# Rotating 96 images by 180 degrees: the third load split into 112 and 16 rows, and a store of the first group tied to it

## The chip, the cores and the metric

The kernel runs on one core of a Trainium2 chip. The metric is the device time of one execution in microseconds; the median of three runs before the change is 121.94 us (121.81 to 122.52).

## The reference

```python
def setup_inputs():
    batch, c, h, w = 32, 3, 256, 256
    return {"x": np.random.randn(batch, c, h, w).astype(np.float32)}

def reference(x):
    return np.rot90(x, k=2, axes=(-2, -1)).astype(np.float32)
```

Each of the 96 images of 256 x 256 floats is turned by 180 degrees. Seen as one row of 65,536 numbers, an image is simply reversed. Nothing is calculated; 25.2 MB are read and 25.2 MB written.

## The kernel before

Every image is cut into four pieces of E = 16,384 numbers (64 KB). The 384 pieces are the rows that the kernel handles, 128 at a time, one to a partition of the on-chip memory. There are three groups (lines 34 and 35): A takes the even pieces of the first 64 images, B the odd ones, C all pieces of the last 32 images. Each group has its own tile of 128 x 16,384 floats, and all three fit at once.

Reversing an image takes two steps. The order of its pieces is reversed by the address pattern of the store (line 54, `::-1`). Inside a piece VectorE reverses the numbers in place: `swap` (lines 56 to 60) exchanges a block of w columns near the front with its mirror image near the back, through the spare tile T, by three copies that read backwards (`back`, line 43). `turn(t, lo, hi)` (line 69) does the swaps for the front columns lo to hi, J = 2048 columns at a time; turning the columns 0 to half = 8192 turns the whole tile. So a tile takes four swaps, twelve copies.

The order of the work is written out by hand. All copies stay in program order on VectorE (line 47). The transfers are issued from two queues: SP issues the loads of A and C and all four stores, in the order written; ACT issues the load of B, after a small clearing of B's first 256 columns by VectorE (line 65), which only delays that load. [...]

- Loads (lines 64 to 67): A on SP, B on ACT, C on SP.
- VectorE turns the columns 0 to 6144 of A (line 76), outermost first. The columns 0 to 256 of A (`LEAD`) are final after the first swap and are stored by a small transfer of 128 KB (line 77).
- Columns 0 to 2560 (`MID`) of B are turned (line 78), then the innermost 2048 of A (line 79). Then the rest of A can be stored (line 80, 8064 KB).
- The rest of B is turned and B stored (lines 81 and 82), then C (lines 83 and 84).

## Time and profile before

| | |
|---|---|
| median of 3 runs | 121.94 us |
| the profiled execution's own time | 121.9 us |
| its span (first to last instruction) | 120.1 us |
| VectorE busy | 44.9 us, 40 instructions |
| DMA | 1008 packets, 50.33 MB |
| VectorE waits for the load of A | 38.3 us |

In the table of slices the span is cut into 40 parts of 3 us; a digit is the busy share in tenths. "DMA" there is the mean of the core's 16 DMA engines. The last part of the page lists the DMA issues: the issuing queue (SPq, ACTq), the size of a store, and the microseconds from the issue to the landing of the last byte. In the timeline each line begins with the start and the length in microseconds; for SPq and ACTq that is the issue alone, not the transfer.

### The profile page before, as it was taken

Reading aid. Unit: us, or ns where it says so; the run is one execution under the profiler, and the core shown is the slowest. Engines: PE = TensorE matmul, PEld = TensorE weight load, DVE = VectorE, ACT = ScalarE, POOL = GpSimd, SP = SyncE. Lnnn points to the kernel's source line nnn. Section 1 sums busy time; section 2 is a strip of 40 time slices with the busy share of each in tenths; the row PEclk is TensorE's granted clock in tenths of the full one; section 3 lists DMA queues with packets and bytes.
Section 4 is the critical chain, followed back from the end, with each engine's and each line's share of the span. In section 5 each row is a group of like instructions: output and inputs, shape, how many; then the busy total and the mean of one; then the engine's idle time right before and its main releaser. Section 6 shows DMA issues by size and latency. Waiting matters only on the chain.

```text
span 120.1 us, 97 instructions
## 1 busy us (share of the span) xinstructions
DVE 44.9 (37%) x40; POOL 0.2 (0%) x4
## 2 busy tenths in 40 slices
DVE  0000000000000899999999999999400000000000
POOL 0000000000000000000000000000000000000000
DMA  9888988898889988998899777988898889888980
GB/s 349 349 349 371 677 349 349 349 698 349 349 349 633 415 349 349 546 502 349 349 387 687 344 344 344 687 349 349 349 698 349 349 349 698 349 349 349 677 371 0
DMA packets 1008, 50.33 MB, mean 419 GB/s; under 512 B 112, under 2 KB 240, under 8 KB 240
## 3 DMA queue, kind: packets, MB, share of 16 engines
q1 hardware_dynamic: 864, 41.94, 81.3%
q10 hardware_dynamic: 144, 8.39, 16.1%
HBM read 25.17 MB, written 25.17 MB: 419 GB/s over the span
## 4 chain that ended last, share of the span: by engine, by line
DVE 38%; DMA 32%; issue 1%
DMA A<-in_x_dram 32%; DVE T L47 13%; DVE Bt L47 9%; DVE A L47 8%; DVE Ct L47 8%
## 5 line engine op out<-in xcount | busy, mean ns | idle before, releaser
L47 DVE COPY T<-A 128x2048 f32<-128x2048 f32 x4 | 4.9, 1226 | 38.4 <-DMA A<-in_x_dram 38.3
L47 DVE COPY T<-Bt 128x2048 f32<-128x2048 f32 (+2 forms) x5 | 5.1, 1014 | 0.2
L47 DVE COPY Bt<-T 128x2048 f32<-128x2048 f32 (+2 forms) x5 | 5.1, 1014 | 0.2
L47 DVE COPY Bt<-Bt 128x2048 f32<-128x2048 f32 (+2 forms) x5 | 5.1, 1013 | 0.2
L47 DVE COPY T<-Ct 128x2048 f32<-128x2048 f32 x4 | 4.9, 1227 | 0.1
L47 DVE COPY Ct<-T 128x2048 f32<-128x2048 f32 x4 | 4.9, 1227 | 0.1
L47 DVE COPY A<-T 128x2048 f32<-128x2048 f32 x4 | 4.9, 1227 | 0.1
L47 DVE COPY A<-A 128x2048 f32<-128x2048 f32 x4 | 4.9, 1227 | 0.1
L47 DVE COPY Ct<-Ct 128x2048 f32<-128x2048 f32 x4 | 4.9, 1226 | 0.1
L65 DVE MEMSET Bt<- 128x256 f32 x1 | 0.3, 272 | 0.9 <-PEq L99 0.9
L99 POOL MEMSET const-bfloat16-1.0<- 128x1 bf16 x1 | 0.1, 102 | 0.0
L99 POOL MEMSET const-uint8-127<- 128x1 uint8 x1 | 0.1, 102 | 0.0
L99 POOL MEMSET const-float32-0.0<- 128x1 f32 x1 | 0.1, 99 | 0.2 <-issue 0.2
L99 POOL MEMSET const-float32-1.0<- 128x1 f32 x1 | 0.1, 99 | 0.0
## 6 DMA issues: line engine op xcount, KB each, us to landing
out_dram<-A SPq DMA_DIRECT2D x1, 8064.0 KB, 20.9
out_dram<-A SPq DMA_DIRECT2D x1, 128.0 KB, 18.4
A<-in_x_dram SPq DMA_DIRECT2D x1, 38.7
Bt<-in_x_dram ACTq DMA_DIRECT2D x1, 43.1
Ct<-in_x_dram SPq DMA_DIRECT2D x1, 60.1
out_dram<-Bt SPq DMA_DIRECT2D x1, 29.6
out_dram<-Ct SPq DMA_DIRECT2D x1, 33.9
```

The costliest lines, as they stand in the source:

```text
L47: tc.keep_in_program_order(nc.vector.tensor_copy(out=dst, in_=src))
L65: nc.vector.memset(Bt[:, 0:256], 0.0)
L99: nc = _bacc.Bacc("TRN2", target_bir_lowering=False, num_devices=1)
```

## The change

```diff
-    MID = 2560
+    R = P - 16
     LEAD = 256
+    LATE = 6144
+    KEY = 128
     load(A, 0, 0, E)
     nc.vector.memset(Bt[:, 0:256], 0.0)
     load(Bt, 1, 0, E, nc.scalar)
-    load(Ct, 2, 0, E)
+    nc.sync.dma_start(out=Ct[0:R, :], in_=x4[2][0:R, :])
+    nc.sync.dma_start(out=Ct[R:P, :], in_=x4[2][R:P, :])
...
-    turn(A, 0, half - J)
+    turn(A, 0, half - KEY)
     store(A, 0, 0, LEAD)
-    turn(Bt, 0, MID)
-    turn(A, half - J, half)
+    turn(Bt, 0, half - LATE)
+    copy(T[0:R, 0:8], back(Ct, 0, 8)[0:R])
+    turn(A, half - KEY, half)
     store(A, 0, LEAD, E)
-    turn(Bt, MID, half)
+    turn(Bt, half - LATE, half)
     store(Bt, 1, 0, E)
```

The load of C becomes two transfers on SP, one behind the other: partitions 0 to 111, then 112 to 127. VectorE now turns all of A but its innermost 128 columns, then one block of 2048 columns of B. Then it copies eight columns of C's first 112 rows into T. Nobody uses these values; the copy can only run once the 112 rows have landed, and since VectorE works in order, what stands behind it waits as well. Behind it come the innermost 128 columns of A, and with them the store of the rest of A. The remaining 6144 columns of B follow. The number of columns turned is the same; the block of 512 columns and that of 1536 in B are gone, and in A there are one of 1920 and one of 128 in place of one of 2048. The stores and the other loads are unchanged.

## The prediction

> **What bounds the kernel now.** I read the page's top first: which of the units is never at rest.

> ```profile
> span 120.1 us, 97 instructions
> DVE 44.9 (37%) x40; POOL 0.2 (0%) x4
> ...
> DVE  0000000000000899999999999999400000000000
> ...
> DMA  9888988898889988998899777988898889888980
> ...
> DMA packets 1008, 50.33 MB, mean 419 GB/s; under 512 B 112, under 2 KB 240, under 8 KB 240
> ```

> VectorE works 44.9 us, in the middle third. The DMA engines are busy in every slice but the last. So the transfers are the bound, and the question for any edit is whether it lengthens them or leaves a hole between them. Next the DMA issues, which say how long each took to land:

> ```profile
> out_dram<-A SPq DMA_DIRECT2D x1, 8064.0 KB, 20.9
> out_dram<-A SPq DMA_DIRECT2D x1, 128.0 KB, 18.4
> A<-in_x_dram SPq DMA_DIRECT2D x1, 38.7
> Bt<-in_x_dram ACTq DMA_DIRECT2D x1, 43.1
> Ct<-in_x_dram SPq DMA_DIRECT2D x1, 60.1
> out_dram<-Bt SPq DMA_DIRECT2D x1, 29.6
> out_dram<-Ct SPq DMA_DIRECT2D x1, 33.9
> ```

> Added to the issue times of the timeline (columns: start, length; the second fence is a closer look at it):

> ```profile
> 0.73 0.38 SPq L50 DMA_DIRECT2D A<-in_x_dram  x1
> ...
> 1.16 0.43 SPq L50 DMA_DIRECT2D Ct<-in_x_dram  x1
> 39.47 1.23 DVE L47 COPY T<-A 128x2048 f32<-128x2048 f32 x1 [38.34 <-DMA A<-in_x_dram]
> ...
> 54.60 0.43 DVE L47 COPY T<-Bt 128x512 f32<-128x512 f32 x1
> ...
> 70.31 0.54 SPq L53 DMA_DIRECT2D out_dram<-Bt  x1
> ...
> 85.45 0.54 SPq L53 DMA_DIRECT2D out_dram<-Ct  x1
> ```

> ```profile
> 59.76 0.55 SPq L53 DMA_DIRECT2D out_dram<-A  x1
> ```

> they give the landings: A 39.4, B 44.3, C 61.3, A's first 256 columns 61.7 (43.25 + 18.4), the rest of A 80.7, B's store 99.9, C's store 119.4. The last two are 19.2 and 19.5 us apart. A group is 128 rows of 64 KB, eight to each of 16 engines, so one row takes one engine 19.35 / 8 = 2.42 us (27.1 bytes per ns); I call that a slot. The program has 384 rows in and 384 out, 48 slots, 116.2 of the 120.1 us; 3.9 us are the start, the end and the small store. The rows of C are the last eight slots of the loads: 61.3 - 8 x 2.42 = 41.9 to 61.3. After them the stores run without a hole: 61.3 to 119.4 is 58.1 us, 24 slots.

> **The change, part by part.** The sum is made against the profiled execution: 121.9 us, of which 1.8 lie around its span of 120.1; the median of the runs is 121.94, the same.

> *One more issue on SP.* It costs 0.38 to 0.43 us at 1.6 us. SP is next needed at 43.25 for the small store, which still depends only on the first swap of A. Cost nothing, covered by 41 us. One more completion mark per engine: the small store's nine packets per engine took about 61.7 - 61.3 = 0.4 us, so a packet costs 0.04 us at most; taken as 0.

> *The order on VectorE.* A wide copy takes 1.23 us, 1.26 with its gap; 2048 columns against 512 are 1.23 against 0.43, so 0.52 us per 1000 columns over 0.16. Three wide swaps of A end at 50.82 as now. The new 1920-column swap is 3 x (1.16 + 0.03) = 3.6, to 54.4; one swap of B, 3 x 1.26, to 58.2. There VectorE now waits for the 112 rows. The small copy has no row of its own size: between 0 and the 0.43 of 512 columns; I take 0.2, near the 0.16 left at no columns. The 128-column swap is 3 x (0.23 + 0.03) = 0.8. So the large store of A is issued 1.0 us after the 112 rows land, or at 59.2 if they are early. Behind the waiting copy stand three swaps of B (11.35 us) and all of C (15.1 us); behind the store on SP stand those of B and C.

> *The 112 rows and the 16.* Seven rows to each engine, then one. If a row costs 2.42 us wherever it goes, they land at 58.8 and 61.3 and nothing is added. But no row shows a transfer that is narrower than 128 partitions, and this decides everything. What the rows do show: load and store run at the same pace, with one queue filled or two, in every full-width transfer. Their common side is the tile memory, and the pace of all 16 engines together, 434 bytes per ns, is nowhere exceeded. [...] The 16 late rows lie side by side. They could use 16 ways (one slot, no cost) or as few as two (eight rows on each, eight slots, 19.4 us). The no-cost end is a rival below; of the shared cases, 8, 4 and 2 ways, I take the middle, four ways with four late rows on each: four slots, 9.7 us instead of 2.42. Then the 12 other ways carry eight rows each of the 112, so these need eight slots instead of seven, however they are dealt out: 61.3 instead of 58.8, and up to a slot more where two engines meet on a way. Together 8 + 4 = 12 slots in place of 8: + 4 x 2.42 = +9.7 us, and the loads end at 70.9. With 8 ways it is 8 + 2 slots, +4.8; with two ways 8 + 8, +19.4. Below nothing it cannot go by more than 0.4 us: rows and bytes are the same, and the only time not filled with them between start and end is around the small store.

> [...]

> *What follows.* The 112 rows land at 61.3 to 63.7, VectorE waits up to 5.5 us from 58.2, and the large store of A is issued at 62.3 to 64.7. Today it lands 20.9 us after its issue, of which eight rows are 19.0 to 19.4: at most 1.9 us for start and landing. It is ready on the engines by 66.6, before the late rows end at 70.9: no further cost, with 4.3 us of cover. If the late rows took a single slot, that cover would be gone. B's store is issued at 64.7 + 11.35 = 76.1 (now 70.31), needed when A's ends at 90.4. C's at 91.2, needed at 109.6. Both stay hidden by over 14 us. The stores take 58.1 us as now.

> Sum: 121.9 + 9.7 = 131.6 us (loads to 70.9, stores to 129.0, span 129.8, 1.8 around it).

> **The rivals.**

> *Not slower: the narrow transfer costs one slot.* If the engine alone sets the pace, the 112 rows land at 58.8, the store of A is issued at 58.84 + 0.02 + 0.2 + 0.8 = 59.86, against 59.76 now. That store has some 0.3 us of room (ready at 61.3 by the bound above, the small store ends at 61.65), so the time stays 121.9 to 122.0. For it: every row in the trace costs 2.42. Against: every row in the trace belongs to a full-width transfer. It decides if the 16 rows land within 2.5 us of the 112.

> *The change doesn't do what it says: the 112 rows land no earlier than all.* If each engine serves fixed partitions, the 16 rows are four rows for each of four engines, the other 12 keep eight of the 112 rows, and no engine has more to do. But the wait opens at 61.3, not 58.8. The store is issued at 62.3, 2.5 us later than now, less the 0.3 of room: +2.2, 124.1 us. For it: the equal pace in all transfers would come just from such a layout. Against: an even split by count is simpler.

> *Rows dealt out in turn.* If neighbouring rows go to neighbouring engines, each wave of 16 rows crowds four ways, all seven waves of the 112 too: 8 waves x 3 extra slots x 2.42 = +58, less what engines gain by falling out of step; 160 to 180 us. Against it: full-width transfers, dealt out so, would be as slow, and are not.

> *Faster.* Only if the small hole around the small store closes: 0.4 us, 121.5. For over 1% there is no room.

> **How the numbers follow.** About 1% (1.2 us) is what a measurement here can tell from no change. Narrow rows share ways: 0.60 (four ways 0.48, eight 0.07, two 0.05), with its own range 126.7 to 141.3. One slot: 0.22. The late wait: 0.10. Dealt in turn: 0.05. Faster by over 1%: 0.03. So slower 0.75, same 0.22, faster 0.03. The range must hold the 0.22 at the low end, so it begins at 121.6; at the high end it takes four ways with a collision more, 134.0, and leaves out two ways, the rows in turn and the gain (0.13).

> **What would show it.** The landings of C's two parts in the DMA issues: 61 to 64 and about 71 as forecast; 58.8 and 61.3 for no cost; both near 61.3 for the late wait. In the slices the DMA rate between 61 and 71 us should fall well under that of the stores. VectorE's wait on the load of C (5 us, or 0.6, or 3) and the issue of A's large store (64, 59.9 or 62.3) tell the same. Wrong would be the forecast if C's second part lands within 3 us of its first.

## The result, and the profile after

The changed kernel takes 142.7 us (median of 6 runs, 142.14 to 143.24) against 121.98 before: a ratio of 1.170, 95% interval 1.168 to 1.172. The forecast was slower, 131.6, with a range of 121.6 to 134.0. The direction and the place are right, the size is off by a factor of two (20.7 us longer, forecast 9.7).

The profiled execution took 143.24 us, with a span of 141.5. The top of its page:

```profile
span 141.5 us, 100 instructions
DVE 45.1 (32%) x41; POOL 0.2 (0%) x4
...
DMA  8696969698999399999591799999989998989980
GB/s 297 297 593 297 593 297 593 297 537 352 463 426 222 74 297 297 297 259 278 93 241 19 267 408 474 401 474 402 463 389 482 408 463 352 500 389 482 408 352 0
DMA packets 1024, 50.33 MB, mean 356 GB/s; under 512 B 128, under 2 KB 256, under 8 KB 256
```

VectorE does the same work as before, the bytes are the same, and the DMA engines still look busy almost throughout. The line of rates shows what happened: from the thirteenth to the twenty-third slice (a slice is 3.54 us here, so some 42 to 81 us) it falls to 300 GB/s and below. The windows view says it without the noise of the slices. Its last three columns are the TensorE clock, the busy share of the DMA engines, and GB/s. After the change, the loads of C's two parts, and the stores:

```profile
41.00:70.00 29.00, 16.78 (x14) 0.00 (x0) 1.00 1.04 251
70.00:83.00 13.00, 6.52 (x9) 0.00 (x0) 1.00 0.98 210
83.00:102.00 19.00, 18.48 (x16) 0.00 (x0) 1.00 1.01 436
```

and before, the whole load of C and the store behind it:

```profile
42.00:61.00 19.00, 18.45 (x17) 0.00 (x0) 1.00 0.97 416
61.60:80.60 19.00, 18.45 (x17) 0.00 (x0) 1.00 1.01 435
```

An engine whose rows take longer counts as just as busy: share 1.04 at 251 GB/s, share 0.97 at 416. The stores run at 436 GB/s, as before (435). The DMA issues, in the close look at the first part's issue, and for all:

```profile
Ct<-in_x_dram SPq DMA_DIRECT2D x1, 74.9
```

```profile
out_dram<-A SPq DMA_DIRECT2D x1, 8064.0 KB, 24.9
out_dram<-A SPq DMA_DIRECT2D x1, 128.0 KB, 39.8
Ct<-in_x_dram SPq DMA_DIRECT2D x2, 78.1
A<-in_x_dram SPq DMA_DIRECT2D x1, 38.8
Bt<-in_x_dram ACTq DMA_DIRECT2D x1, 46.1
out_dram<-Bt SPq DMA_DIRECT2D x1, 32.8
out_dram<-Ct SPq DMA_DIRECT2D x1, 37.0
```

and the timeline:

```profile
1.19 0.41 SPq L69 DMA_DIRECT2D Ct<-in_x_dram  x1
1.64 0.43 SPq L70 DMA_DIRECT2D Ct<-in_x_dram  x1
...
57.00 1.23 DVE L47 COPY Bt<-T 128x2048 f32<-128x2048 f32 x1
76.20 0.17 DVE L47 COPY T<-Ct 112x8 f32<-112x8 f32 x1 [17.98 <-DMA Ct<-in_x_dram]
...
88.54 0.54 SPq L53 DMA_DIRECT2D out_dram<-Bt  x1
...
103.67 0.54 SPq L53 DMA_DIRECT2D out_dram<-Ct  x1
```

```profile
77.19 0.55 SPq L53 DMA_DIRECT2D out_dram<-A  x1
```

The 112 rows land at 1.19 + 74.9 = 76.1. The median of two is their mean, so the other load of C took 2 x 78.1 - 74.9 = 81.3 and landed at 82.9. The stores land at 102.1, 121.3 and 140.7. Before, the load of C ended at 61.3 and the last store at 119.4. So the loads end 21.6 us later and everything behind them 21.3 us later: next to nothing is lost or won after the load of C. VectorE waits 18 us for the 112 rows, and what stands behind the small copy waits with it: B has been there since 47.3, and its next swap begins at 77.20. The large store of A is issued 1.0 us after the 112 rows land, at 77.19; its rows wait for those of C anyway, and begin at 79.5 to 82.0 by the packet records (the trace's own record of each row's transfer).

### The profile page after: what moved, and what is told of

Read it like the earlier page. It is cut to its first block, busy times and chain, and to the rows that moved or that the text cites. A ratio compares the mean times of both kernels' runs of the same rounds, so it can differ in the third digit from the quotient of the medians.

```text
span 141.5 us, 100 instructions
## 1 busy us (share of the span) xinstructions
DVE 45.1 (32%) x41; POOL 0.2 (0%) x4
## 2 busy tenths in 40 slices
DMA packets 1024, 50.33 MB, mean 356 GB/s; under 512 B 128, under 2 KB 256, under 8 KB 256
## 3 DMA queue, kind: packets, MB, share of 16 engines
q1 hardware_dynamic: 880, 41.94, 82.9%
## 4 chain that ended last, share of the span: by engine, by line
DVE 32%; DMA 27%; another core or an unknown queue 13%; issue 1%; DVEq 0%
DMA A<-in_x_dram 27%; DVE T L47 11%; DVE A L47 7%; DVE Bt L47 7%; DVE Ct L47 7%; DVEq L47 0%
## 5 line engine op out<-in xcount | busy, mean ns | idle before, releaser
L47 DVE COPY T<-A 128x2048 f32<-128x2048 f32 (+2 forms) x5 | 5.1, 1014 | 38.6 <-DMA A<-in_x_dram 38.4
L47 DVE COPY T<-Ct 128x2048 f32<-128x2048 f32 (+1 forms) x5 | 5.1, 1016 | 18.1 <-DMA Ct<-in_x_dram 18.0
L47 DVE COPY A<-A 128x2048 f32<-128x2048 f32 (+2 forms) x5 | 5.1, 1014 | 0.2
L47 DVE COPY A<-T 128x2048 f32<-128x2048 f32 (+2 forms) x5 | 5.1, 1013 | 0.2
L47 DVE COPY Ct<-T 128x2048 f32<-128x2048 f32 x4 | 4.9, 1227 | 0.1
L47 DVE COPY Bt<-Bt 128x2048 f32<-128x2048 f32 x4 | 4.9, 1227 | 0.1
L47 DVE COPY Bt<-T 128x2048 f32<-128x2048 f32 x4 | 4.9, 1227 | 0.1
L47 DVE COPY T<-Bt 128x2048 f32<-128x2048 f32 x4 | 4.9, 1227 | 0.1
L47 DVE COPY Ct<-Ct 128x2048 f32<-128x2048 f32 x4 | 4.9, 1226 | 0.1
## 6 DMA issues: line engine op xcount, KB each, us to landing
out_dram<-A SPq DMA_DIRECT2D x1, 8064.0 KB, 24.9
out_dram<-A SPq DMA_DIRECT2D x1, 128.0 KB, 39.8
Ct<-in_x_dram SPq DMA_DIRECT2D x2, 78.1
Bt<-in_x_dram ACTq DMA_DIRECT2D x1, 46.1
```

The costliest lines, as they stand in the source:

```text
L47: tc.keep_in_program_order(nc.vector.tensor_copy(out=dst, in_=src))
```

## The experiments

The theory at the start: the narrow transfers are slow because rows meet on shared ways into the tile memory (a way is the prediction's word for a path that a few partitions have in common; no run shows one, and that there are 16, as in the prediction and the expectations, is the author's assumption). The rivals: the source side or the mere number of transfers, and the wait on VectorE with the store behind it. All the kernels that are timed are compared with the kernel before on the same chip.

**Undoing one half and doing the other.** First the split alone:

```diff
-    load(Ct, 2, 0, E)
+    R = P - 16
+    nc.sync.dma_start(out=Ct[0:R, :], in_=x4[2][0:R, :])
+    nc.sync.dma_start(out=Ct[R:P, :], in_=x4[2][R:P, :])
```

> The kernel before, with the load of C as two transfers of 112 and 16 rows and nothing else: no wait for the 112 rows, the old order on VectorE. Theory: all the loss is the transfers' own, so 142.7 us as the full change, within 0.5. Rival, the wait on VectorE and the late store are what costs: 122 to 125 us.

Measured: 142.51 us, ratio 1.169 (1.167 to 1.171). The split alone is the whole loss. There the large store of A is issued at 59.87, 17 us earlier than in the changed kernel, and that buys next to nothing (0.2 us).

Then the wait and the new order alone, against the changed kernel:

```diff
-    R = P - 16
+    R = P
...
-    nc.sync.dma_start(out=Ct[0:R, :], in_=x4[2][0:R, :])
-    nc.sync.dma_start(out=Ct[R:P, :], in_=x4[2][R:P, :])
+    load(Ct, 2, 0, E)
```

> The changed kernel with the load of C in one full-width transfer again: VectorE's small copy waits for all of C, and the order of the swaps is the new one. Theory: the load ends at 61.3, the store of A is issued 1.0 us later at 62.3 instead of 59.76, 0.3 of that is covered: 124.1 us. Rival, the wait and the order cost the 20 us: over 140.

Measured: 124.62 us, ratio 1.023 (1.020 to 1.026), 0.5 us over the sum. Its timeline:

```profile
61.42 0.17 DVE L47 COPY T<-Ct 128x8 f32<-128x8 f32 x1 [3.17 <-DMA Ct<-in_x_dram]
...
62.40 0.54 SPq L53 DMA_DIRECT2D out_dram<-A  x1
```

The store is issued 2.64 us later than before (62.40 against 59.76), and the kernel is 2.64 us slower (124.62 against 121.98). The 0.3 us of room that the prediction gave to that store do not show; late is late, one for one. It is near the 124.1 that the prediction's rival of a late wait had named as its price.

**The same change with full-width parts.** The load of C split by columns:

```diff
-    nc.sync.dma_start(out=Ct[0:R, :], in_=x4[2][0:R, :])
-    nc.sync.dma_start(out=Ct[R:P, :], in_=x4[2][R:P, :])
+    load(Ct, 2, 0, 7 * J)
+    load(Ct, 2, 7 * J, E)
```

> The changed kernel with the load of C split by columns instead of rows: 14336 columns of all 128 partitions, then 2048 columns of all 128; the small copy waits for the first part. Same number of transfers, same wait, and an eighth of the bytes in the late part, but both parts fill all partitions. Theory: width is the cause, so parts land at 58.8 and 61.3 and the time is 121.9 to 122.5. Rival, a second transfer or the wait behind it is the cause whatever its width: over 140.

Measured: 122.11 us, ratio 1.001 (1.000 to 1.002). Two transfers, the wait and the late eighth are all there, and the loss is gone:

```profile
Ct<-in_x_dram SPq DMA_DIRECT2D x1, 7168.0 KB, 57.6
Ct<-in_x_dram SPq DMA_DIRECT2D x1, 1024.0 KB, 59.9
```

Issued near 1.2 and 1.6, they land at 58.8 and 61.5, as the prediction had it for transfers that cost one slot a row. So neither a second transfer nor the wait behind it costs anything that shows. What is left of the change is the width of the parts.

**The transfers by themselves.** A kernel that only loads, one transfer after the other (it ran once, under the profiler):

```python
def probe(name, first, count, step, source=xs):
    t = pool.tile([P, E], x.dtype, tag="R", name=name)
    last = first + (count - 1) * step + 1
    nc.sync.dma_start(out=t[first:last:step, :], in_=source[0:count, :])
```

> This kernel leaves out the rotation: it only loads, one transfer after the other, each waiting for the one before, thirteen transfers of whole 64 KB rows that differ in how many partitions they fill and which; every time it gives is the landing of one of them. [...] Rival, the source side: the pace follows from how many rows a transfer has or where they lie in the input; then all four 16-row transfers take the same time, and the 112 rows that are read from other places of the input take another time than the first 112. Rival, eight neighbours to a way: every eighth partition takes 1 slot (2.4), 16 neighbours 8 slots (19.4).

Its DMA issues (the last number is the time from issue to landing; "otherrows" is 112 low partitions filled from every second row of another part of the input, "highhundredtwelve" the partitions 16 to 127):

```profile
full<-in_x_dram SPq DMA_DIRECT2D x1, 21.9
...
lowhundredtwelve<-in_x_dram SPq DMA_DIRECT2D x1, 31.9
highhundredtwelve<-in_x_dram SPq DMA_DIRECT2D x1, 34.2
otherrows<-in_x_dram SPq DMA_DIRECT2D x1, 32.4
lowninetysix<-in_x_dram SPq DMA_DIRECT2D x1, 32.0
lowsixtyfour<-in_x_dram SPq DMA_DIRECT2D x1, 22.9
midsixtyfour<-in_x_dram SPq DMA_DIRECT2D x1, 12.4
lowthirtytwo<-in_x_dram SPq DMA_DIRECT2D x1, 12.3
lowsixteen<-in_x_dram SPq DMA_DIRECT2D x1, 11.8
highsixteen<-in_x_dram SPq DMA_DIRECT2D x1, 11.7
everyeighth<-in_x_dram SPq DMA_DIRECT2D x1, 7.5
everyfourth<-in_x_dram SPq DMA_DIRECT2D x1, 7.3
everysecond<-in_x_dram SPq DMA_DIRECT2D x1, 12.5
```

The full load takes 21.9 for eight slots of 2.42, so 2.5 us are start and landing. Now read the lines in pairs: 64 rows in the partitions 0 to 63 take 22.9, the same 64 rows in 32 to 95 take 12.4. 16 neighbours take 11.8, 16 at every eighth partition 7.5. The source rows are the same in each pair, so it is the place in the tile memory that counts; and where the source alone is changed (31.9 and 32.4) next to nothing happens. That rules out the source side. Eight neighbours to a way fails too: every eighth partition would then have taken one slot, and took two (7.5 - 2.5 = 5.0 us).

**What is wrong with 112 rows.** Two explanations were tried: rows that meet slow only each other, and the rows are dealt to the engines in some bad way; or rows that meet slow all.

> As the first measuring kernel (no rotation, transfers one by one), with other widths and strides. Open is why 112 and 96 rows take 30 us where 8 slots on the fullest way would be 20. Theory one, lockstep: each engine gets consecutive rows (7 of 112, 6 of 96), and where two rows that are moved at the same time share a way, all 16 engines are slowed, not those two alone. Then of the 16 rows at every seventh partition (two pairs share a way, twelve rows have their own) all 16 take about 4.8 us, and so do those at every sixth; at every third (up to three on a way) all take about 7.2; 48 rows take 9 slots (21.8 us), 80 rows 10 slots (24.2), beside 2 us of start and landing. Theory two, no lockstep, and the rows are dealt to the engines in another way (first the lowest 64, four to each engine, then the rest): then at every seventh partition twelve rows take 2.4 us and four take 4.8, at every sixth ten and six, and 80 rows take 16 slots less drift or so (four of 4.8 us and one of 9.7, 29 us).

In transfers of 16 rows each engine has one row (in the changed kernel's trace the 16 late rows run side by side, one behind each engine's last row of the 112), so there is no question how they are dealt. From the packet records, the shortest and the longest of the 16 rows, with the ways by the grouping inferred above. The measure is the first row on each engine in the full load, 2.5 to 3.5 us; its later rows took 2.42.

```
partitions       most on a way, rows with a way to themselves    us of one row
every fifth      2, six                                          4.3 to 5.3
every sixth      2, ten                                          4.1 to 5.0
every seventh    2, twelve                                       4.1 to 5.0
every eighth     2, none                                         4.5 to 5.2
every third      3, three                                        6.3 to 7.5
16 neighbours    4, none                                         7.1 to 9.3
```

At every seventh partition two pairs meet by that grouping, and the twelve rows that meet nobody are as slow as the four: all 16 took 4.1 to 5.0 us. At every third the three lone rows take at least 6.3 us. So in these transfers rows that meet hold up those that meet nobody, and all 16 engines go near the pace of the fullest way. That is what is called lockstep here.

The wider transfers follow:

```profile
lowfortyeight<-in_x_dram SPq DMA_DIRECT2D x1, 26.8
loweighty<-in_x_dram SPq DMA_DIRECT2D x1, 27.3
lowninetysix<-in_x_dram SPq DMA_DIRECT2D x1, 32.1
```

As an estimate from the slot of 2.42, with consecutive rows to each engine, lockstep gives 9 slots (21.8 us) for 48 rows, 10 (24.2) for 80, 12 (29.0) for 96 and 14 (33.9) for 112. Less the 2.5 they measure 24.3, 24.8, 29.6 and 29.4 to 31.7. Rows that slow only those they meet, followed step by step with the same grouping and consecutive rows, give 19 to 24 for all four. 48 rows are above their lockstep sum (with three on a way their rows took up to 8.4 us, more than three slots) and 112 below it.

The packet records show why 112 rows fall below. By the grouping and with consecutive rows, two pairs meet while the engines move their first three rows and their last two, but only one pair during the fourth and during the fifth. In the changed kernel's trace the first three rows took 4.3 to 4.9 us on every engine, the last two 4.3 to 6.0. The fourth took 4.8 on two engines and 2.8 to 3.3 on the other fourteen, the fifth 4.2 and 4.6 on two and 3.5 to 3.6 on fourteen. The split alone shows the same. So lockstep is not all or nothing in these rows: where one pair meets by the grouping, the other engines are slowed, but not to half pace (2.8 to 3.6 us where a row of a full load takes 2.42); where two pairs meet, all 16 go at about half (4.3 to 4.9 in the first three rows).

**Lockstep in the kernel.** Another uneven split, without a wait, as a test of the numbers:

```diff
-    load(Ct, 2, 0, E)
+    R = 80
+    nc.sync.dma_start(out=Ct[0:R, :], in_=x4[2][0:R, :])
+    nc.sync.dma_start(out=Ct[R:P, :], in_=x4[2][R:P, :])
```

> The kernel before with the load of C as 80 and 48 rows, no wait for a part. Lockstep (all 16 engines go at the pace of the fullest way): from the transfers measured alone, 80 rows take 24.2 to 25.5 us and 48 rows 21.8 to 25.3, together 46.0 to 50.8 in place of 19.35: 148.6 to 153.4 us. Rival, only the rows that meet are slowed, so that the fullest way sets the sum: 8 rows on a way and then 6, 33.9 us, 136.5.

Measured: 151.81 us, ratio 1.244 (1.242 to 1.247): +29.9, inside the lockstep numbers, and 15 us over the rival's. With consecutive rows that slow only those they meet, 80 and then 48 rows would take at most 21.8 + 19.4 us, 143.8 in all; the kernel is 8 us over that too.

**Splits of equal size, different partitions.** Two parts of 64 rows, even and odd, or lower and upper:

```diff
-    load(Ct, 2, 0, E)
+    nc.sync.dma_start(out=Ct[0:P:2, :], in_=x4[2][0:P:2, :])
+    nc.sync.dma_start(out=Ct[1:P:2, :], in_=x4[2][1:P:2, :])
```

> The kernel before with the load of C as two transfers of 64 rows, the even partitions and then the odd ones; old order, no wait for a part. Theory of the ways: every second partition reaches all 16 ways with four rows each, so both parts run at full pace, 122.0 to 122.3 us. Rival, a transfer that is narrower than 128 rows is slow as such: 130 or more.

Measured: 121.96 us, ratio 1.000 (0.999 to 1.001).

```diff
-    load(Ct, 2, 0, E)
+    R = P // 2
+    nc.sync.dma_start(out=Ct[0:R, :], in_=x4[2][0:R, :])
+    nc.sync.dma_start(out=Ct[R:P, :], in_=x4[2][R:P, :])
```

> The same with the lower 64 partitions and then the upper 64: two transfers of the same sizes as the even and odd ones, only other partitions. Theory of the ways: each half reaches eight ways only, four rows per engine at 5.1 us each, 41 us in place of 19.4: +21.6, 143.6 us. Rival, the size of the parts decides: as the even and odd split.

Measured: 143.29 us, ratio 1.175 (1.173 to 1.176). The same bytes in the same two sizes: one split is free, the other costs 21.3 us. So a narrow transfer is not slow as such: 64 even rows kept the pace.

**The whole change with a split that spreads.**

```diff
-    R = P - 16
+    R = 1
...
-    nc.sync.dma_start(out=Ct[0:R, :], in_=x4[2][0:R, :])
-    nc.sync.dma_start(out=Ct[R:P, :], in_=x4[2][R:P, :])
+    nc.sync.dma_start(out=Ct[0:P:2, :], in_=x4[2][0:P:2, :])
+    nc.sync.dma_start(out=Ct[1:P:2, :], in_=x4[2][1:P:2, :])
```

R is left only in the small copy, which now reads one row of the even part.

> The changed kernel with its new order and its small copy, but the load of C is split into the even and the odd partitions, 64 rows each, and the small copy (here of one row) waits for the even ones. Theory: with transfers that reach all 16 ways the rest of the change costs nothing: the even rows land at 51.7, the small copy waits for nothing, the store of A is issued at 59.2, and the time is 121.9 to 122.3. Rival: the change's order or small copy has a cost of its own that was hidden behind the slow loads: over 123.

Measured: 121.95 us, ratio 1.000 (0.998 to 1.001). The order, the small copy and the store tied to it cost nothing, and bring nothing.

**What the moment of the store is worth.**

```diff
-    MID = 2560
+    MID = 0
```

> The kernel before with MID = 0: A is turned without a break and its large store is issued at 54.6 us instead of 59.76, seven us before the loads end. No part of the change; it asks whether the moment of that store, which the change ties to the load, is worth anything as long as it isn't late. Theory: the store's rows stand behind those of C on the same queue and change nothing, 122.0 us (121.6 to 122.1, the smaller if the short hole before the store's rows closes). Rival: a store that is queued early disturbs the loads, 123 or more.

Measured: 122.97 us, ratio 1.008 (1.006 to 1.009), practically the rival's 123: a store queued this early costs 1.0 us. Its store and its load of C:

```profile
54.63 0.54 SPq L53 DMA_DIRECT2D out_dram<-A  x1
```

```profile
Ct<-in_x_dram SPq DMA_DIRECT2D x1, 61.0
```

0.9 later than the 60.1 before. By the packet records it is the last row of C on each engine, the one right before the store's, which takes 3.28 us on average (3.06 to 3.46) instead of 2.42; all rows before it are as they were. So the moment matters: 5 us too early costs 1.0 us, 2.6 us too late costs 2.6. The kernel before issues the store in between, and the versions of the change with wide parts (59.86 with the columns, 59.28 with even and odd) measure the same. None beats it.

## Why the prediction was right and wrong

- *The transfers are the bound, and the edit is worth what it does to them*: right. The loads end 21.6 us later, the last store 21.3.
- *Four ways with four late rows on each, four slots*: the time came out: 16 neighbours alone take 9.3 us beside start and landing, against 9.7 in the sum. Four was taken as the middle of three cases, a choice and not a reading of the trace. No run shows the ways that the sum counts, 16 of them with eight rows on each; what the runs showed in their place are times, 9.3 us for 16 neighbours, 5.0 for 16 rows at every eighth partition, and 34 in the kernel for the 112 rows. In the kernel the two landings are 82.9 - 76.1 = 6.8 us apart, because engines that finish their part of the 112 early begin the 16 early (from 70.5 to 74.4 us, by the packet records).
- *"so these need eight slots instead of seven, however they are dealt out: 61.3 instead of 58.8, and up to a slot more where two engines meet on a way"*: wrong, and this is the step that failed. The 112 rows landed at 76.1. Measured from the prediction's 41.9 they took 34 us in place of the 19.4 to 21.8 of the sum. The prediction let the fullest way set the total, as if engines with a way to themselves went on at full pace meanwhile. The runs showed lockstep: where two pairs of the rows that move at the same time meet by the inferred grouping, every engine took 4.1 to 5.0 us for its row, also the twelve that meet nobody. If the engines take consecutive rows, five of the seven rows of the 112 are moved beside two such pairs and the other two beside one, which slowed the others to 2.8 to 3.6 us.
- In terms of the sum: of the +21.6, the 112 rows are 76.1 - 58.8 = +17.3 (forecast +2.4 to +4.9), the 16 rows 6.8 - 2.5 = +4.3 (forecast +7.3). The highest value that was given for shared ways, +19.4 for two ways, would have been nearly the size, but by another cause.
- *"Wrong would be the forecast if C's second part lands within 3 us of its first"*: the sign did not show, the parts land 6.8 us apart, and the forecast failed all the same. The sign watched the 16 rows, and most of the loss lay in the 112.
- *The split's issue, the order on VectorE, the small copy*: right. The small copy took 0.17 us (0.2 forecast), the 128-column copies 0.23, the store is issued 1.0 us after the landing, and the even and odd version shows all of it at no cost.
- *The store of A is covered by the late rows*: right; it was issued at 77.2 and its rows began at 79.5 to 82.0, behind those of C. The split alone, with that store at 59.87, is as slow.
- *A late store costs what it is late, less 0.3 of room*: the room was not there (2.64 for 2.64).
- *The chances*: the rival at no cost (0.22) rested on the equal pace of all rows in the trace. That pace says nothing of a width that the trace does not hold.

The strides show that rows which meet hold up others in a load from the main memory (4.1 to 5.0 us for all 16 rows at every seventh partition); which piece of the path holds the other engines up, no run here shows.

Open remains in which order an engine takes its rows. Consecutive rows fit the times of 48, 80, 96 and 112 rows, and which rows of the 112 ran faster, but would make the rows of the even partitions, and of a full load, meet in pairs by the same grouping, and both ran at full pace (12.5 us for 64 rows, 21.9 for 128). That rows which meet nobody are held up does not hang on it: in the transfers of 16 rows each engine has only one.

## What to carry to other kernels

Ask of a split by partitions which partitions each part fills, not only how many: split by columns (122.11 us), or into even and odd partitions (121.96), and the parts kept the pace of the whole here; the lower 48, 64, 80, 96 or 112 partitions did not, and 112 rows took longer than 128 (31.9 us against 21.9). Contiguous alone is not the trouble: the 64 partitions from 32 to 95 kept the pace (12.4 us). Where the transfers are the bound, read the rate beside the busy share: the changed kernel's engines are shown as busy at 251 GB/s as at 436. And price a shared resource for all its users, not only for those that meet on it, until a run shows that the others go on.

## What the runs showed of the hardware

- 16 rows, one on each engine, took 4.1 to 5.0 us each at every sixth or seventh partition, where the first rows of a full load took 2.5 to 3.5; at every third partition 6.3 to 7.5, and as 16 neighbours 7.1 to 9.3.
- 112 rows of 64 KB in the lower partitions took 31.9 us where 128 took 21.9, and the lower 48 took 26.8, nearly as long as the lower 80 (27.3).
- A transfer's completion mark waited behind a row of the other queue. The load of B, untouched by the change, is shown as landing after 46.1 us instead of 43.1: by the packet records its last rows ended as before (41.0 to 41.6 us, before 41.0 to 41.5), and its marks stand behind the first rows of C, at 45.4 to 46.4 us instead of 43.4 to 43.9; those rows now take 4.3 to 4.8 us instead of 2.42.
- A store issued at 54.6 us, on the same queue and 7 us before the load ahead of it ended, stretched the last row of that load from 2.42 to 3.28 us; issued at 59.8 (the kernel before) it didn't.
